# Two-layer hybrid decoder trunk: q first and four tiles wide, sixteen MLP tiles on unnormalised input, and 512-column matmuls that join the two halves of x in the last layer

## The chip, the cores and the metric

The kernel runs on one core of a Trainium2 chip. The time is the device time of one execution in microseconds (us); three executions of the kernel before were timed. One more execution was taken with the hardware profiler, and all rows below come from it.

## The reference, cut to what matters

Sixteen meta tokens and 256 tokens (272 positions, 2048 wide, float32) are normalised and go through two layers. The meta tokens are dropped at the end, so that the last layer computes 256 positions where it can.

```python
def hybrid_layer(h, ...):
    z = h @ in_proj                                   # 2048 x 6656
    q, k, v, u, g = split(z)                          # 1024, 256, 256, 1024, 4096 columns
    g_attn, g_ssm = split(sigmoid(g + gate_b))
    y_attn = sliding_window_attention(q, k, v, bias, sinks)
    y_ssm = s5_mixer(u, ...)                          # scan over time, gelu, y * sigmoid(y @ w_glu)
    mixed = (g_attn * (y_attn @ w_attn_up) + g_ssm * (y_ssm @ w_ssm_up)) @ w_out
    h = layer_norm(DN_ALPHA * h + mixed, ln_mix_g, ln_mix_b)
    f = square(relu(h @ w_mlp_up)) @ w_mlp_down       # 2048 -> 8192 -> 2048
    return layer_norm(DN_ALPHA * h + f, ln_mlp_g, ln_mlp_b)
```

## The kernel before, in words

Activations lie transposed: a tile holds 128 features on the partitions and the positions along the free axis, 16 tiles `H0..H15` for a width of 2048. To keep float32 accuracy with the faster matmul type, each operand is split in a rounded high part and the low rest. A product is three matmuls that add up in one PSUM bank: high weights by high x, high weights by low x, low weights by high x. The high and the low part of x lie in one tile, a row of positions apart.

`gemm` (line 408) cuts a product into steps. A step loads 512 KB of weights (1024 columns per partition) on SP's queue, ScalarE copies the high part `wh`, VectorE subtracts it from the loaded weights to get the low part `wo` (`split`, line 368), and TensorE runs 24 matmuls. Three pairs `wh`, `wo` are in turn, so that the split for a step begins when TensorE has left the step three before it. `wide` is how many output tiles of 128 features one group of steps fills: with 2, a step covers two output tiles and four of the contraction tiles k; with 4, four output tiles and two k. All output tiles of a group keep a bank until the last k. When an output tile is complete, its `evac` generator empties the bank, and the bank is free again when the generator's first reader has been issued (`self.free(p)`).

Six banks go round among the products (`BANKS`), and up to three of them may be held by side work, attention and the state-space branch (`SIDE`). The order of instructions on every engine is written out by a planner at build time: each piece of work is a generator that says on which engine and when it could go on (estimated times), the planner takes the earliest, and evacuations go before weight splits, weight splits before layer norm and side work.

The products of a layer, in order: u (line 1472 or 1474, four wide), k, q, v (1498 to 1500, two wide), the attention gate (1516), attn_up (1527), 28 of 32 steps of the state-space gate `gs` (1526), glu (1548), the rest of `gs`, ssm_up (1563, four wide), w_out (1582), and for each half of the 8192 hidden features mlp_up (1605, 1607, 1612, four wide) and mlp_down (in the last layer `down_tok`, line 1664, with tokens as weights and 512 columns of w_mlp_down as the moving operand). Attention runs beside the attention gate and must be over before attn_up; the state-space branch runs beside it from u on and must be over before glu.

Two layer norms are hidden behind products on unnormalised input. `ln_add` makes tiles `XG` of x times the norm's gain before the statistics are there, u of the second layer and the first eight tiles of mlp_up read these, and `deferred` (928) repairs their output with the statistics afterwards: a multiplication, which frees the bank, and an addition on VectorE. Meanwhile `ln_put` (910) writes the sixteen normalised tiles, each with two VectorE passes, a high copy on ScalarE and a low subtraction on VectorE. The product after it waits for these tiles one by one.

In the last layer `residual_tok` (1644) turns the residual to token order with 32 transposes and eight ScalarE copies; it starts a new pair only while at most two banks are held (line 1650), and `down_tok` lets it finish at line 1672.

Of the kernel before, what the change touches and what calls it, by code (L numbers as in the profile page):

```python
# [14 lines left out]
ALU = mybir.AluOpType  # L15
# [7 lines left out]
KT = D // 128  # L23
# [5 lines left out]
C_Q, C_K, C_V, C_U, C_GA, C_GS = 0, 1024, 1280, 1536, 2560, 4608  # L29
# [7 lines left out]
NCH = FF // 2 // 128  # L37
# [11 lines left out]
def fr(t, off, dims):  # L49
    return bass.AP(t.tensor, t.offset + off, [list(t.ap[0])] + [list(d) for d in dims])  # L50
# [131 lines left out]
class Builder:  # L182
# [222 lines left out]
        yield  # L405


    def gemm(self, w, c0, ms, nk, xs, n, evac, wide=2, r0=0, pre=None):

        steps, ms = [], list(ms)  # L410
        for g in range(0, len(ms), wide):
            group = ms[g:g + wide]
            ku = 8 // len(group)
            ps = {}
            for k0 in range(0, nk, ku):
                r, c = r0 + 128 * k0, c0 + 128 * group[0]
                src = w[r:r + 128 * ku, c:c + 128 * len(group)].rearrange("(k p) c -> p k c", p=128)

                def need(k0=k0, ku=ku):
                    for k in range(k0, k0 + ku):  # L420
                        xs(k)

                def mm(whi, wlo, k0=k0, ku=ku, ps=ps, group=group):
                    for j, m in enumerate(group):
                        if k0 == 0:
                            ps[m] = self.psum()
                        p, c = ps[m][:, :n], slice(128 * j, 128 * j + 128)
                        for i in range(ku):
                            k = k0 + i
                            hi, lo = xs(k)  # L430
                            self.mm(p, whi[:, i, c], hi, k == 0, False)
                            self.mm(p, whi[:, i, c], lo, False, False)
                            self.mm(p, wlo[:, i, c], hi, False, k == nk - 1)
                        if k == nk - 1:
                            self.own(evac(m, p), self.FIRST, p)

                steps.append(Step(src, (ku, 128 * len(group)), mm, need, pre if not steps else None))
        return steps
# [998 lines left out]
    def layer(self, l, prev):  # L1437
        nc, V, A, a = self.nc, self.V, self.A, self.a
        last = l == DEPTH - 1
        T0 = N_META if last else 0  # L1440
        n = NT - T0
        ts = slice(T0, NT)
        xh = lambda k: (self.H[k][:, 0, :NT], self.H[k][:, 1, :NT])
        xt = lambda k: (self.H[k][:, 0, ts], self.H[k][:, 1, ts])
        w_in = a["in_proj"][l]
        ctx = {}
        steps = []
# [45 lines left out]
        def ev_q(m, p):  # L1493
            yield self.after("act")
            A.activation(out=q_tile(m)[:, 0, ts], in_=p, func=AF.Copy, scale=0.125)
            self.free(p)

        steps += self.gemm(w_in, C_K, range(2), KT, xh, NT, ev_k)
        steps += self.gemm(w_in, C_Q, range(8), KT, xt, n, ev_q)
        steps += self.gemm(w_in, C_V, range(2), KT, xh, NT, ev_v)  # L1500

        def attn_go():
# [4 lines left out]
        def ev_gate(store, base, gm):  # L1507
            def ev(m, p):
                yield self.after("act")
                if m // 2 not in store:  # L1510
                    store[m // 2] = self.t(f"{base[0]}{base[1] + m // 2}", [128, 2, NT])
                A.activation(out=store[m // 2][:, m % 2, ts], in_=p, func=AF.Tanh, bias=self.gate_b(l, gm + m), scale=0.5)
                self.free(p)
            return ev

        steps += self.gemm(w_in, C_GA, range(16), KT, xt, n, lambda m, p: ev_gate(self.GA, ("G", 0), 0)(m, p), pre=attn_go)

        ya = lambda k: (self.Y[k][:, 0, ts], self.Y[k][:, 1, ts])

# [82 lines left out]
        for c in range(2):  # L1602
            w_up = a["w_mlp_up"][l]
            if c == 0:
                steps += self.gemm(w_up, 0, range(8), KT, lambda k: self.xg(self.ln)(k), n + 2,
                                   lambda m, p: self.deferred(self.ln, ev_up2)(m, p), 4)
                more = self.gemm(w_up, 0, range(8, NCH), KT, xt, n, ev_up2, 4)
                if last:
                    more[0].pre = lambda: ctx.__setitem__("rt", self.start(self.residual_tok(XS, self.ln, ctx)))
                steps += more  # L1610
            else:
                steps += self.gemm(w_up, 4096, range(NCH), KT, xt, n, ev_up2, 4)
            clear = HID.clear
            if not last:
                def ev_down(m, p, c=c):
                    yield self.after("dve")
                    x = XS[m // 2][:, m % 2, :n]
                    if c == 0:
                        V.scalar_tensor_tensor(out=x, in0=x, scalar=ALPHA, in1=p, op0=ALU.mult, op1=ALU.add)
                        self.free(p)  # L1620
                    else:
                        if m == 0:
                            self.ln_begin(1, l, T0)
                        V.tensor_tensor(out=x, in0=x, in1=p, op=ALU.add)
                        self.free(p)
                        yield from self.ln_add(m, x)

                down = self.gemm(a["w_mlp_down"][l], 0, range(16), NCH, hid, n, ev_down, 2 if c else 4, r0=4096 * c)
                if c == 0:
                    down[16].pre = lambda: self.start(self.phase_table(l + 1))  # L1630
            else:
                down = self.down_tok(a["w_mlp_down"][l], l, c, hid, ctx)
            if c == 0:
                down[-1].mm = (lambda hi, lo, f=down[-1].mm: (f(hi, lo), clear()))
            steps += down
# [8 lines left out]
    def residual_tok(self, XS, s, ctx):  # L1644
        R = ctx["res"] = {}
        while s.get("done", 0) < KT:
            yield W
        for c in range(4):
            for t in range(2):
                while t == 0 and (self.room(self.banks, 2) is None or len(self.banks.held) > 2):  # L1650
                    yield W
                yield self.after("pe")
                p = ctx["rp", t] = self.psum(True)
                for j in range(4):
                    x = XS[2 * c + j // 2][:, j % 2, 128 * t:128 * t + 128]
                    self.P.transpose(p[:, 128 * j:128 * j + 128], x, self.ident)
            for t in range(2):
                yield self.after("act")
                p = ctx["rp", t]
                R[c, t] = self.t(f"G{2 * c + t}", [128, 512])  # L1660
                self.A.activation(out=R[c, t], in_=p, func=AF.Copy, scale=ALPHA)
                self.free(p)
# [163 lines left out]
```

## Time and profile before

| | us |
|---|---|
| median of 3 runs | 2728.31 (2727.61 to 2731.21) |
| profiled execution | 2727.87 |
| span of the profile, first to last instruction | 2725.8 |
| TensorE busy | 2686.1 (99%) |
| VectorE busy | 1856.8 (68%) |
| ScalarE busy | 1275.8 (47%) |
| mean granted TensorE clock | 0.997 |

PE is TensorE, PEld its weight loads, DVE VectorE, ACT ScalarE, POOL GpSimd and SP the queue that issues the loads. All instructions come from helpers, so that the line is L147 throughout and rows are told apart by the tiles' names: `wl` is a loaded weight tile, `wh` and `wo` its high and low part, `bank` a PSUM bank, `H` and `D` activation tiles (in the second layer the names of some are swapped), `G` gates and residual, `lnr` and `lnc` the statistics of a layer norm. A matmul's duration contains its pipeline; the pace of a stage is its length divided by its matmuls.

### The profile page before, as it was taken

The numbers are of one execution on the slowest core, as the hardware profiler recorded it, in microseconds if no ns is written. First come the engines' busy times: TensorE is split into PE (matmuls) and PEld (weight loads), VectorE is DVE, ScalarE is ACT, GpSimd is POOL, SyncE is SP. The second block draws the span as 40 slices with busy tenths as digits, with TensorE's granted clock in tenths as the row PEclk, the third lists the DMA queues.
The fourth block names the chain that finished last, engine by engine and source line by source line (L and its number), as shares of the span: only waits on it lengthen the run. The fifth ranks groups of instructions, "written<-read, shape, count | busy, mean of one in ns | idle before, by whom it ended". The sixth has DMA issues, their size and how long they took to land.

```text
span 2725.8 us, 52091 instructions
## 1 busy us (share of the span) xinstructions
PE 2686.1 (99%) x21234; PEld 2581.9 (95%) x21234; DVE 1856.8 (68%) x3293; ACT 1275.8 (47%) x2020; POOL 66.1 (2%) x143
## 2 busy tenths in 40 slices
PE   7999999999999999999999999999999999999997
PEld 6999999999999999999999989999999988999886
DVE  7889985678655766555568999457886544455545
ACT  4456444456543334444445564444565533444433
POOL 2200000000000000000004000000000000000000
PEclk9999999999999999999999999999999999999999
DMA  5654445555664666555556654555566555556653
GB/s 178 181 166 132 150 155 172 176 176 165 178 177 172 197 202 194 176 173 175 175 167 195 191 154 158 181 186 186 186 181 177 176 188 190 186 186 186 217 191 141
DMA packets 378775, 483.36 MB, mean 177 GB/s; under 512 B 49046, under 2 KB 240232, under 8 KB 378536
## 3 DMA queue, kind: packets, MB, share of 16 engines
q1 hardware_dynamic: 374440, 477.81, 55.8%
q8 instruction: 166, 2.72, 0.4%
q0 software_dynamic: 4096, 2.24, 0.3%
q14 instruction: 73, 0.60, 0.1%
HBM read 471.14 MB, written 6.60 MB: 175 GB/s over the span
## 4 chain that ended last, share of the span: by engine, by line
PE 97%; DVE 1%; ACT 1%; SPq 0%; issue 0%; DMA 0%; ACTq 0%; DVEq 0%
PE bank L147 97%; PE pair L147 1%; DVE G L147 0%; SPq L147 0%; ACT wh L147 0%; DVE D L147 0%; DMA D<-in_x 0%; DVE wo L147 0%; ACT H L147 0%; ACT fnw L147 0%; DVE H L147 0%; DVE fst L147 0%; ACT fro L147 0%; DVE erw L147 0%; DVE est L147 0%
## 5 line engine op out<-in xcount | busy, mean ns | idle before, releaser
L147 DVE TENSOR_TENSOR wo<-wl,wh 128x1024 fp32r<-128x1024 f32 x864 | 1056.3, 1224 | 811.3 <-ACT wh L147 803.5
L147 ACT CAST wh<-wl 128x1024 fp32r<-128x1024 f32 x864 | 906.8, 1050 | 1284.4 <-PE bank L147 1094.4
L147 PE MATMUL bank<-D,wh 128*128 128x256 f32 (+2 forms) x7296 | 1347.5, 286 | 4.9 <-DVE D L147 3.5
L147 PEld LDWEIGHTS bank<-D,wh 128*128 128x128 f32 x7296 | 1134.7, 189 | 11.1 <-DVE D L147 4.8
L147 PE MATMUL bank<-D,wo 128*128 128x256 f32 (+2 forms) x3648 | 1039.4, 285 | 0.0
L147 PE MATMUL bank<-H,wh 128*128 128x272 f32 (+3 forms) x4480 | 847.4, 289 | 0.0
L147 PEld LDWEIGHTS bank<-H,wh 128*128 128x128 f32 x4480 | 702.6, 189 | 4.5 <-ACT wh L147 1.0
L147 PEld LDWEIGHTS bank<-D,wo 128*128 128x128 f32 x3648 | 688.2, 189 | 0.0
L147 PE MATMUL bank<-H,wo 128*128 128x272 f32 (+3 forms) x2240 | 644.3, 288 | 0.0
L147 PEld LDWEIGHTS bank<-H,wo 128*128 128x128 f32 x2240 | 423.1, 189 | 0.0
L147 PE MATMUL bank<-wh,D 128*128 128x512 f32 x512 | 161.9, 395 | 0.0
L147 PE MATMUL bank<-wh,H 128*128 128x512 f32 x512 | 161.3, 394 | 0.0
L147 PEld LDWEIGHTS bank<-wh,D 128*128 128x128 f32 x512 | 96.2, 188 | 23.0
L147 PEld LDWEIGHTS bank<-wh,H 128*128 128x128 f32 x512 | 96.2, 188 | 22.2
L147 DVE TENSOR_TENSOR D<-D,D 128x272 f32<-128x272 f32 (+2 forms) x208 | 102.5, 509 | 1.3
L147 PE MATMUL bank<-wo,D 128*128 128x512 f32 x256 | 101.0, 394 | 0.0
L147 PE MATMUL bank<-wo,H 128*128 128x512 f32 x256 | 100.7, 393 | 0.0
L147 POOL DMA_DIRECT2D D<-D x128 | 63.0, 499 | 1404.9 <-ACT D L147 1392.1
L147 ACT ACTIVATE tmp<-bank 128x272 f32<-128x272 f32 (+1 forms) x128 | 49.8, 389 | 19.3 <-PE bank L147 18.6
L147 PEld LDWEIGHTS bank<-wo,D 128*128 128x128 f32 x256 | 48.1, 188 | 11.2
L147 PEld LDWEIGHTS bank<-wo,H 128*128 128x128 f32 x256 | 48.1, 188 | 11.2
L147 DVE TENSOR_TENSOR_SCAN D<-par,D 128x136 f32<-128x136 f32 x128 | 50.7, 427 | 0.6
(245 smaller groups left out, 1473.5 us busy)
## 6 DMA issues: line engine op xcount, KB each, us to landing
wl<-in_w_mlp_up SPq DMA_DIRECT2D x256, 512.0 KB, 3.7
wl<-in_w_mlp_down SPq DMA_DIRECT2D x256, 512.0 KB, 3.5
wl<-in_in_proj SPq DMA_DIRECT2D x208, 512.0 KB, 3.7
wl<-in_w_out SPq DMA_DIRECT2D x64, 512.0 KB, 3.3
wl<-in_w_attn_up SPq DMA_DIRECT2D x32, 512.0 KB, 3.3
wl<-in_w_ssm_up SPq DMA_DIRECT2D x32, 512.0 KB, 3.9
wl<-in_ssm_w_glu SPq DMA_DIRECT2D x16, 512.0 KB, 3.9
turns<-bias SPq DMA_DIRECT2D x16, 272.0 KB, 4.4
```

Of the source, the lines that this page charges most:

```text
L147: return fn(*a, **k)
```

## The change

1. `gemm` gets a flag `join`. Where it is on and n is 256 (only in the last layer), one matmul of 512 columns multiplies the high weights by the high and the low x together, into the left and the right half of a bank; the low weights by the high x still go to the left half. `joined` then copies the right half to a temporary tile on ScalarE and adds it to the left half on VectorE, in the bank, before the evacuation begins. q and the attention gate have the flag off; u, k, v and the early mlp_up tiles have other widths.
2. q comes before k, and four tiles wide instead of two, in both layers.
3. In the last layer sixteen instead of eight tiles of mlp_up are taken on unnormalised input.
4. `residual_tok` starts a pair in the first half of a group (`self.phase` is the share of k that is done), no longer by the number of banks held.

```diff
-    def gemm(self, w, c0, ms, nk, xs, n, evac, wide=2, r0=0, pre=None):
+    def gemm(self, w, c0, ms, nk, xs, n, evac, wide=2, r0=0, pre=None, join=True):
+        both = join and 2 * n == 512
+
+        def joined(m, p, q):
+            yield self.after("act")
+            t = self.tmp()[:, :n]
+            self.A.copy(t, q)
+            yield self.after("dve")
+            self.V.tensor_tensor(out=p, in0=p, in1=t, op=ALU.add)
+            self.free(t)
+            yield from evac(m, p)
...
+                    self.phase = k0 / nk
...
                             hi, lo = xs(k)
-                            self.mm(p, whi[:, i, c], hi, k == 0, False)
-                            self.mm(p, whi[:, i, c], lo, False, False)
+                            if both:
+                                two = fr(hi, 0, [[lo.offset - hi.offset, 2], [1, n]])
+                                self.mm(ps[m].rearrange("p (a b) -> p a b", a=2), whi[:, i, c], two, k == 0, False)
+                            else:
+                                self.mm(p, whi[:, i, c], hi, k == 0, False)
+                                self.mm(p, whi[:, i, c], lo, False, False)
                             self.mm(p, wlo[:, i, c], hi, False, k == nk - 1)
                         if k == nk - 1:
-                            self.own(evac(m, p), self.FIRST, p)
+                            self.own(joined(m, p, ps[m][:, n:2 * n]) if both else evac(m, p), self.FIRST, p)
...
+        steps += self.gemm(w_in, C_Q, range(8), KT, xt, n, ev_q, 4, join=False)
         steps += self.gemm(w_in, C_K, range(2), KT, xh, NT, ev_k)
-        steps += self.gemm(w_in, C_Q, range(8), KT, xt, n, ev_q)
         steps += self.gemm(w_in, C_V, range(2), KT, xh, NT, ev_v)
...
-        steps += self.gemm(w_in, C_GA, range(16), KT, xt, n, lambda m, p: ev_gate(self.GA, ("G", 0), 0)(m, p), pre=attn_go)
+        steps += self.gemm(w_in, C_GA, range(16), KT, xt, n, lambda m, p: ev_gate(self.GA, ("G", 0), 0)(m, p), pre=attn_go, join=False)
...
-                steps += self.gemm(w_up, 0, range(8), KT, lambda k: self.xg(self.ln)(k), n + 2,
+                early = 16 if last else 8
+                steps += self.gemm(w_up, 0, range(early), KT, lambda k: self.xg(self.ln)(k), n + 2,
                                    lambda m, p: self.deferred(self.ln, ev_up2)(m, p), 4)
-                more = self.gemm(w_up, 0, range(8, NCH), KT, xt, n, ev_up2, 4)
+                more = self.gemm(w_up, 0, range(early, NCH), KT, xt, n, ev_up2, 4)
...
-                while t == 0 and (self.room(self.banks, 2) is None or len(self.banks.held) > 2):
+                while t == 0 and (self.room(self.banks, 2) is None or self.phase > 0.5):
```

## Rows read from the trace of the kernel before

**Rows 1.** The page's first part: busy us of each engine, share, instructions.
```profile
PE 2686.1 (99%) x21234; PEld 2581.9 (95%) x21234; DVE 1856.8 (68%) x3293; ACT 1275.8 (47%) x2020; POOL 66.1 (2%) x143
```

**Rows 2.** Windows, one stage each: from:to length, busy us, clock, DMA, GB/s.
```profile
81.11:93.19 12.08, 12.08 (x98) 12.08 (x97) 10.17 (x32) 4.88 (x6) 11.27 (x24) 1.00 0.67 207
...
1453.58:1471.91 18.33, 15.35 (x98) 13.86 (x97) 14.65 (x29) 9.71 (x18) 15.82 (x33) 0.91 0.68 184
...
1730.92:1810.77 79.85, 79.85 (x674) 79.85 (x673) 34.73 (x29) 34.98 (x41) 0.00 (x0) 1.00 0.60 185
...
1844.83:1890.20 45.37, 45.37 (x387) 45.37 (x385) 33.08 (x56) 22.02 (x31) 0.00 (x0) 1.00 0.55 185
1890.20:1981.42 91.22, 91.22 (x773) 91.17 (x771) 74.14 (x126) 46.06 (x78) 0.00 (x0) 1.00 0.57 186
...
2028.39:2171.88 143.49, 141.58 (x1186) 140.83 (x1185) 89.50 (x133) 77.62 (x127) 0.00 (x0) 1.00 0.61 181
2171.88:2350.08 178.20, 178.20 (x771) 144.36 (x770) 81.90 (x72) 69.18 (x70) 0.00 (x0) 1.00 0.54 186
2350.08:2532.90 182.82, 182.82 (x1538) 182.82 (x1536) 98.64 (x124) 86.08 (x123) 0.00 (x0) 1.00 0.59 185
```

**Rows 3.** Timeline of TensorE, k of the second layer: start, us, instruction, [idle, releaser].
```profile
1461.13 0.39 PE L147 MATMUL bank<-D,wh 128*128 128x272 f32 x1 [0.57 <-ACT D L147]
1462.43 0.39 PE L147 MATMUL bank<-D,wh 128*128 128x272 f32 x1 [0.91 <-DVE D L147]
...
1469.35 0.66 PE L147 MATMUL bank<-D,wh 128*128 128x272 f32 x2
...
1470.03 0.66 PE L147 MATMUL bank<-D,wh 128*128 128x272 f32 x2
```

**Rows 4.** Windows of 3 us in the same stage, columns as in rows 2.
```profile
1469.00:1472.00 3.00, 3.00 (x15) 3.00 (x16) 0.29 (x1) 0.39 (x1) 2.61 (x7) 0.55 1.07 237
```

**Rows 5.** Timeline of VectorE: low parts of normalised tiles, and a repair of u.
```profile
1434.57 0.79 DVE L147 TENSOR_TENSOR D<-G,D 128x272 fp32r<-128x272 f32 x2
...
1452.68 0.43 DVE L147 TENSOR_TENSOR tmp<-bank,lnr 128x272 f32<-128x272 f32 x1
...
1457.61 0.44 DVE L147 TENSOR_TENSOR D<-G,D 128x272 fp32r<-128x272 f32 x1
...
1461.94 0.79 DVE L147 TENSOR_TENSOR D<-G,D 128x272 fp32r<-128x272 f32 x2
...
1468.24 0.44 DVE L147 TENSOR_TENSOR D<-G,D 128x272 fp32r<-128x272 f32 x1 [0.48 <-ACT D L147]
```

**Rows 6.** Timeline of TensorE, mlp_up of the last layer.
```profile
2043.05 0.38 PE L147 MATMUL bank<-D,wh 128*128 128x256 f32 x1 [0.20 <-ACT D L147]
...
2045.82 0.39 PE L147 MATMUL bank<-D,wh 128*128 128x256 f32 x1 [1.13 <-DVE D L147]
```

**Rows 7.** Timeline of VectorE: the last normalised tiles of that norm.
```profile
2050.61 0.76 DVE L147 TENSOR_TENSOR D<-G,D 128x256 fp32r<-128x256 f32 x2
```

**Rows 8.** Groups by form, ScalarE: count | busy us, mean ns of one | idle before.
```profile
L147 ACT ACTIVATE tmp<-bank 128x256 f32<-128x256 f32 x64 | 24.4, 382 | 8.6 <-PE bank L147 8.5
```

**Rows 9.** Groups by form, VectorE.
```profile
L147 DVE SCALAR_TENSOR_TENSOR G<-G,bank 128x256 f32<-128x256 f32 x16 | 6.7, 418 | 2.0 <-PE bank L147 2.0
```

**Rows 10.** Timeline of ScalarE where one group of four follows another (mlp_up).
```profile
2371.11 0.38 ACT L147 ACTIVATE tmp<-bank 128x256 f32<-128x256 f32 x1
...
2373.00 1.05 ACT L147 CAST wh<-wl 128x1024 fp32r<-128x1024 f32 x1 [0.21 <-PE bank L147]
```

**Rows 11.** Timeline of VectorE at the same place.
```profile
2371.24 1.23 DVE L147 TENSOR_TENSOR wo<-wl,wh 128x1024 fp32r<-128x1024 f32 x1 [1.62 <-ACT wh L147]
```

**Rows 12.** Attention's last products, by tile: count, ns min/median/max, first and last start.
```profile
L147 PE MATMUL bank<-H,vab x96: 272/273/324, 1569.7 to 1642.1; 128*64 128x128 f32 x96
```

**Rows 13.** The chain in order of time: the state-space branch's last input product.
```profile
1680.67 0.67 PE pair L147 x8
```

**Rows 14.** Groups by form, TensorE: the residual's transposes.
```profile
L147 PE MATMUL bank<-ident,G 128*128 128x128 f32 x32 | 3.7, 272 | 0.0
```

## The prediction, made before the change was built

> **What bounds the kernel now.** I read the page first, then windows laid on the stages, then the timeline where a stage is longer than its matmuls, last the rows of the two engines that feed TensorE. TensorE is busy for 2686 of 2725.8 us and VectorE for 68% [rows 1]: the time is the sum of matmuls, so I count matmuls and look for places where TensorE stands.
>
> A stage's length over its matmuls is the pace. With 256 columns, 28 steps of the state-space gate take 79.85 us for 672 matmuls (118.8 ns), ssm_up 45.37 for 384 (118.2), w_out 91.22 for 768 (118.8), the second mlp_up 182.82 for 1536 (119.0). With 512 columns, the first mlp_down of the last layer takes 178.20 us for 768 (232.0) [rows 2]. I use 118.7 and 232.0: 256 more columns cost 113.3 ns, so 256 columns cost 113.3 and each matmul some 5.4 ns more, whatever its width.
>
> TensorE stands in two places. k of the second layer takes 18.33 us, k of the first, the same 96 matmuls, 12.08 [rows 2]: 6.25 us are lost. The timeline shows how: matmuls wait for a normalised tile (0.57 us, 0.91 us, and so on) [rows 3], and then the granted clock is 0.55 for 3 us [rows 4], three matmuls taking 0.68 us (1469.35 to 1470.03) [rows 3], about twice their usual time; that is the level of 1.2 instead of 2.4 GHz after the idling. The second place is mlp_up of the last layer, where the first tiles on normalised input wait 0.20 and 1.13 us and once more between them [rows 6]. That stage has 1152 matmuls (137.1 us at 119.0) and 32 transposes (3.7 us) [rows 14], 140.8 of 143.49 [rows 2]: 2.7 us lost.
>
> **Part 1, joined matmuls.** Joined products in the last layer are gate 16 tiles by 16 k, attn_up 16 by 8, glu 8 by 8, ssm_up 16 by 8, w_out 16 by 16, mlp_up 16 by 16 and 32 by 16: 256 + 128 + 64 + 128 + 256 + 256 + 512 = 1600 pairs. Each pair of 256-column matmuls (237.4 ns) becomes one of 512 (232.0): 5.4 ns, in all 8.7 us less. No row shows a moving operand in two pieces; mlp_down's is one piece. Bounds: if the break costs as much as a matmul's start, nothing is gained; if each of the two pieces pays a start, 8.6 us are lost; if all 12 ns that a 256-column matmul takes beyond 256 columns at 2.4 GHz (106.7) go, 19 us are gained. I take 8.7, from the nearest row, 512 columns into the same kind of bank.
>
> The Trainium skill, page "TensorE: Matmul & The Clock Gate", section "Wait — 56ns, not 53.3ns?", puts the fixed cost of a warm matmul at 2.5 ns on top of its columns at 2.4 GHz. By it the 1600 pairs would give 4.0 us instead of 8.7, and the total below would be 2717.7. These rows disagree: 118.7 and 232.0 ns stand 12.0 and 18.7 above such columns [rows 2], so the measured paces decide.
>
> **What the join adds.** 16 + 16 + 8 + 16 + 16 + 16 + 32 = 120 tiles get a ScalarE copy of 256 columns, priced by its nearest row, an evacuation from a bank, 0.38 us [rows 8], and a VectorE addition, 0.42 us [rows 9] (bounds 0.3 to 0.8 us, as no row shows VectorE writing to a bank): 46 and 50 us of engine time. It lies beside matmuls. VectorE is busy 33.08 of 45.37 us in ssm_up and 74.14 of 91.22 in w_out [rows 2]; with 16 additions each (6.7 us) 39.8 of some 44.7 and 80.8 of some 89.8. These are the tightest stages, and the matmuls still last longer. At 0.8 us an addition ssm_up would hold VectorE 45.9 us, over 1 us too long.
>
> What can go late is a bank. With groups of four, two of six banks are free when a group ends; the new group's third tile needs that of the old group's first. In the second mlp_up the first group ends at 2350.08 + 192 x 0.119 = 2372.93, the third tile starts 12 matmuls on, at 2374.36. The old first tile was read at 2371.11, bank free at 2371.49 [rows 10]: 2.9 us early. Afterwards a copy (0.38) is done by 2371.49; the addition stands behind a split that runs from 2371.24 to 2372.47 [rows 11], so is done by about 2372.9; the read competes with a copy of weights at 2373.00 (1.05 us) [rows 10]. Ahead of it, the bank is free at 2373.3; behind it, at 2374.4, just late. There are 3 such boundaries in ssm_up, 3 in the joined part of the first mlp_up, 7 in the second: 13. I take 0.15 us each, 2 us; bounds 0 and 0.4 us each (5 us).
>
> **Part 2, q first, four wide.** k used four new tiles in 3 us; q uses two per step of 24 x 0.1187 = 2.85 us. After u ends at 1453.58 [rows 2], tile 11 (k = 10) is needed at step 5, 1467.8, tile 13 at 1470.7, tile 15 at 1473.5. The low parts, counted in order, give the tenth at 1458.05 (first and last of seven such rows shown), 11 and 12 at 1462.73, the sixteenth at 1468.68 [rows 5]: all 5 us early. So stall and half clock go: 6.25 us. k then finds all tiles. q needs four banks at once where u has just ended; its third tile starts 12 matmuls on, at 1455.0, and u's second bank is released at 1453.1 [rows 5], so nothing waits. Loads: q has 16 steps of 512 KB either way, in rows twice as long, moved past k's four loads on SP's queue, and issues nothing on POOL's; v and the attention start stay where they were, as the three products take the same time together. In the first layer k runs at full pace (12.08 us) [rows 2], so order alone gives nothing. Held banks rise from two to four during q, leaving two for side work; that hides in attention's end at 1642.1 [rows 12] against attn_up, which starts 384 x 0.1187 = 46 us before the state-space gate's 1730.92 [rows 2], near 1685, and in the branch's last input product at 1681 [rows 13] against glu after 1810.77 [rows 2]. Without that cover, each microsecond late would be one of the path. Bounds 0 and 6.25 us.
>
> **Part 3, sixteen early tiles.** They run some 46 us longer on unnormalised input, until about 2074; the last normalised tiles are ready at 2051.4 [rows 7]. The 2.7 us go. Eight tiles by 48 = 384 matmuls are 258 wide instead of 256: 2 x 0.443 x 384 = 0.3 us. Their repair, two more VectorE passes on each of eight tiles (0.42 each [rows 9]), 7 us, hides in that stage's 54 idle VectorE us [rows 2]. Bounds 0 and 2.7.
>
> **Part 4, residual.** 32 transposes come earlier and stay as many; their 3.7 us [rows 14] are paid there as here. Their two banks in the first half of a group hinder nothing that the second half needs. Zero, bounds -0.5 and +0.5.
>
> **Sum.** -8.7 - 6.25 - 2.7 + 0.3 + 2.0 = -15.35 us. The profiled execution took 2727.87 (span 2725.8 and 2.1 around it), the median is 2728.31, 0.4 more: 2712.5 and 2713.0. I say 2713.
>
> **Rivals.** (B) *Two pieces cost two starts*: the join pays nothing, the stalls go all the same. For it: no row has a moving operand in pieces; against: nothing in the rows charges for pieces, and 512 columns run at 232. 2713 + 8.7 = 2721.7.
> (D) *The normalised tiles stay late*: VectorE follows u's repairs, so that the tiles shift with q. For it: VectorE is busy 14.65 of 18.33 us there [rows 2]; against: 5 us of reserve. 2713 + 6.25 = 2719.3.
> (C) *The bank takes the stall's place*, slower than before: at each of the 13 boundaries the addition stands behind a split and the read behind a copy of weights, and both again because other tiles' passes come first. One split and one copy beyond the reserve are 1.23 + 1.05 = 2.28 us [rows 10, 11], at 13 boundaries 30 us: 2713 - 2 + 30 = 2741. It decides from (15.35 + 2.0) / 13 = 1.3 us a boundary. For it: one such pair uses up the reserve already; against: evacuations go ahead of splits in the planner.
> (E) *All the overhead goes with the matmul*: 19.2 us instead of 8.7, 2702.5.
>
> **How the numbers follow.** What a measurement here can tell from no change is 0.2%, 5.5 us, so faster means below 2722.8. Chances: forecast 0.56 (0.53 faster, 0.03 same), B 0.14 (half and half, as it lies at the bound), D 0.12 (0.11 and 0.01), E 0.08, C 0.10 (0.09 slower, 0.01 same). Faster 0.79, same 0.12, slower 0.09. The range takes E in below and reaches past B above, with the banks' 5 us and the worse bounds in part: 2702 to 2725.
>
> **What would show it.** Right: in the last layer a pair of 512 and 256 columns every 350 ns; q of the second layer starts with no wait, and no window at half clock before the end; mlp_up's first normalised tile without a wait; at 13 boundaries gaps under half a microsecond. Wrong: a 512-column matmul in the joined products above 237 ns (B) or below 226 (E); waits of q on tiles of layer norm (D); idle time before a group's third tile, released by ScalarE or VectorE reading a bank (C); or new waits of TensorE on attention, which I leave as they are.

## The result and the profile after

The changed kernel takes 2714.42 us (median of 6 runs, 2713.35 to 2716.49), the kernel before 2729.43; the ratio is 0.9945, 95% interval 0.9932 to 0.9958. Forecast were 2713 and 15.35 us less; the medians differ by 15.0. The profiled execution took 2714.52 us, its span is 2712.7, 13.1 less than the span before.

The page's first part answers to [rows 1]: 1600 matmuls fewer, VectorE and ScalarE each some 40 us busier.

```profile
PE 2679.0 (99%) x19634; PEld 2503.7 (92%) x19634; DVE 1898.5 (70%) x3421; ACT 1315.7 (49%) x2156; POOL 66.3 (2%) x143
```

Windows of the changed kernel by stage of the last layer, each from its first matmul to the next stage's first; columns as in [rows 2]. In order: q, k, v, attention gate, attn_up, 28 steps of the state-space gate, ssm_up, w_out, the sixteen early mlp_up tiles, the other sixteen, the first mlp_down, the second mlp_up (glu and the last steps of the gate, between 1803.38 and 1837.04, are left out).

```profile
1454.77:1506.24 51.47, 51.21 (x458) 50.14 (x457) 45.60 (x93) 28.28 (x51) 15.86 (x33) 1.00 0.71 207
1506.24:1521.27 15.03, 15.03 (x164) 14.21 (x162) 13.92 (x28) 7.37 (x14) 0.00 (x0) 1.00 0.61 172
1521.27:1536.09 14.82, 14.82 (x154) 14.17 (x148) 14.50 (x29) 6.67 (x12) 0.00 (x0) 1.00 0.59 187
1536.09:1676.39 140.30, 139.40 (x1423) 129.91 (x1419) 132.22 (x370) 80.54 (x199) 0.00 (x0) 1.00 0.60 166
1676.39:1724.82 48.43, 48.43 (x347) 41.81 (x346) 43.93 (x82) 24.23 (x38) 0.00 (x0) 1.00 0.55 173
1724.82:1803.38 78.56, 78.56 (x450) 68.63 (x449) 39.95 (x44) 38.34 (x54) 0.00 (x0) 1.00 0.61 188
1837.04:1881.93 44.89, 44.89 (x259) 39.30 (x258) 36.86 (x67) 26.79 (x46) 0.00 (x0) 1.00 0.59 185
1881.93:1972.18 90.25, 90.25 (x516) 78.93 (x515) 79.78 (x145) 51.70 (x95) 0.00 (x0) 1.00 0.61 188
1972.18:2065.29 93.11, 93.11 (x775) 93.00 (x773) 80.16 (x147) 63.54 (x124) 0.00 (x0) 1.00 0.63 182
2065.29:2159.67 94.38, 94.38 (x547) 82.16 (x546) 55.91 (x80) 53.35 (x92) 0.00 (x0) 1.00 0.63 179
2159.67:2337.80 178.13, 178.13 (x771) 144.26 (x770) 85.88 (x82) 69.90 (x73) 0.00 (x0) 1.00 0.61 189
2337.80:2519.76 181.96, 181.96 (x1025) 157.37 (x1024) 107.99 (x152) 93.54 (x151) 0.00 (x0) 1.00 0.64 185
```

The stages of the kernel before that [rows 2] does not hold: q, v, attention gate, attn_up, eight early tiles.

```profile
1471.91:1527.01 55.10, 55.10 (x537) 52.92 (x535) 49.58 (x104) 27.12 (x50) 0.00 (x0) 1.00 0.63 183
1527.01:1542.13 15.12, 15.12 (x164) 14.30 (x162) 14.80 (x29) 6.51 (x14) 0.00 (x0) 1.00 0.59 172
1542.13:1684.23 142.10, 140.03 (x1447) 130.07 (x1442) 135.79 (x376) 80.45 (x196) 0.00 (x0) 1.00 0.57 163
1684.23:1730.92 46.69, 46.69 (x426) 46.36 (x425) 32.19 (x49) 18.36 (x20) 0.00 (x0) 1.00 0.55 181
1981.42:2028.39 46.97, 46.97 (x391) 46.86 (x389) 40.73 (x76) 30.98 (x60) 0.00 (x0) 1.00 0.63 180
```

The reader is to take sums over stages that end at the same matmul, since side work moves between neighbours:

| stretch | before | after | difference |
|---|---|---|---|
| up to the end of u, second layer | 1453.58 | 1454.77 | +1.2 |
| q, k, v, attention gate, attn_up | 277.34 | 270.05 | -7.3 |
| state-space gate to w_out | 250.50 | 247.36 | -3.1 |
| first mlp_up | 190.46 | 187.49 | -3.0 |
| mlp_down, second mlp_up, mlp_down | 539.13 | 538.44 | -0.7 |
| after the last matmul starts | 14.8 | 14.6 | -0.2 |

The +1.2 is the first product (u of the first layer), which starts beside the first loads: it took 59.7 to 60.9 us over all the profiles here, whatever the order of q and k. No other stage of the first layer differs by more than 0.6 us.

### The profile page after: what moved, and what is told of

Same layout as the page of the kernel before. It is cut to its first block, busy times and chain, and to the rows that moved or that the text cites. A ratio compares the mean times of both kernels' runs of the same rounds, so it can differ in the third digit from the quotient of the medians.

```text
span 2712.7 us, 49216 instructions
## 1 busy us (share of the span) xinstructions
PE 2679.0 (99%) x19634; PEld 2503.7 (92%) x19634; DVE 1898.5 (70%) x3421; ACT 1315.7 (49%) x2156; POOL 66.3 (2%) x143
## 4 chain that ended last, share of the span: by engine, by line
PE 98%; DVE 0%; ACT 0%; SPq 0%; DMA 0%; issue 0%; ACTq 0%
PE bank L147 97%; PE pair L147 1%; DVE G L147 0%; SPq L147 0%; DMA D<-in_x 0%; ACT fnw L147 0%; ACT H L147 0%; DVE D L147 0%; DVE fst L147 0%; ACT fro L147 0%; ACT vm L147 0%; ACT wh L147 0%; DVE erw L147 0%; DVE est L147 0%; ACT frs L147 0%
## 5 line engine op out<-in xcount | busy, mean ns | idle before, releaser
L147 PE MATMUL bank<-D,wh 128*128 128x272 f32 (+3 forms) x5696 | 1293.8, 314 | 0.0
L147 PE MATMUL bank<-D,wo 128*128 128x256 f32 (+2 forms) x3520 | 1002.3, 285 | 0.0
L147 PEld LDWEIGHTS bank<-D,wh 128*128 128x128 f32 x5696 | 933.8, 189 | 65.4 <-ACT tmp L147 2.2
L147 PE MATMUL bank<-H,wh 128*128 128x272 f32 (+3 forms) x4480 | 893.9, 296 | 0.0
L147 PEld LDWEIGHTS bank<-H,wh 128*128 128x128 f32 x4480 | 712.6, 189 | 15.8 <-ACT wh L147 1.0
L147 PE MATMUL bank<-H,wo 128*128 128x272 f32 (+3 forms) x2368 | 680.9, 288 | 0.0
L147 PEld LDWEIGHTS bank<-D,wo 128*128 128x128 f32 x3520 | 663.3, 188 | 0.1
L147 PEld LDWEIGHTS bank<-H,wo 128*128 128x128 f32 x2368 | 448.1, 189 | 0.0
L147 PEld LDWEIGHTS bank<-wo,D 128*128 128x128 f32 x256 | 48.1, 188 | 11.6 <-DVE wo L147 0.4
L147 ACT COPY tmp<-bank 128x256 f32<-128x256 f32 x120 | 44.5, 371 | 16.1 <-PE bank L147 15.1
```

Source lines behind the costliest of these rows:

```text
L147: return fn(*a, **k)
```

## The experiments

Each edit is made to the changed kernel. Most stages repeat to some 0.05 us between profiles of kernels that don't differ there; u of the first layer, q and the attention gate of the second and the last mlp_down differ by 0.4 to 1.2 us. So stages tell apart what the whole time, which scatters by 1 to 2 us, cannot.

**The join off.**

```diff
-        both = join and 2 * n == 512
+        both = False
```

> The changed kernel with the join off everywhere: three 256-column matmuls per pair again, no copy and addition; q first, the sixteen early tiles and the residual's test stay. Theory (each removed matmul saves its fixed 5.4 ns, 1600 of them, and the additions cost some 2 us in bank waits): 8.7 - 2 = 6 to 7 us slower than the changed kernel, about 2721, and no gap before the third tile of a group in mlp_up. Rival (two pieces cost two starts, the gain came from the stalls alone): within 2 us of the changed kernel. Rival (the additions cost more than the join gains): faster than the changed kernel.

Measured: 2721.27 us (2718.8 to 2722.0), 0.9967 of the kernel before (0.9954 to 0.9979). Windows of the second mlp_up, of the attention gate, and of 3 us within the gate:

```profile
2343.87:2526.70 182.83, 182.83 (x1538) 182.82 (x1537) 98.61 (x124) 86.07 (x123) 0.00 (x0) 1.00 0.61 185
1535.92:1678.49 142.57, 141.19 (x1423) 131.46 (x1420) 132.31 (x370) 80.40 (x199) 0.00 (x0) 0.99 0.59 163
...
1546.00:1549.00 3.00, 3.00 (x14) 3.00 (x15) 2.96 (x12) 0.38 (x2) 0.00 (x0) 0.50 1.01 268
```

The whole is 6.8 us slower, as the theory has it, but 2.3 of that is the attention gate, which is not joined: TensorE waits 0.35 and then 0.50 us before matmuls of attention near its start, where the changed kernel has only the first wait, and the clock then goes to half (0.50 above; 1.00 throughout in the changed kernel). Over the joined stages the join gives 4.9 us: state-space gate 79.84 to 78.56 and 11.39 to 11.23, attn_up 48.82 to 48.43, glu 22.67 to 22.43, ssm_up 45.37 to 44.89, w_out 91.22 to 90.25, first mlp_up 94.91 to 94.38, second 182.83 to 181.96. Per pair that is 5.7 ns in the gate (224 pairs), 3.75 in ssm_up and w_out, only 1.7 in the second mlp_up.

**q after k, two wide.**

```diff
+        steps += self.gemm(w_in, C_K, range(2), KT, xh, NT, ev_k)
+        steps += self.gemm(w_in, C_Q, range(8), KT, xt, n, ev_q, join=False)
-        steps += self.gemm(w_in, C_Q, range(8), KT, xt, n, ev_q, 4, join=False)
-        steps += self.gemm(w_in, C_K, range(2), KT, xh, NT, ev_k)
```

> The changed kernel with q after k and two wide again, as before. Theory (k of the second layer catches up with the normalised tiles, idles and loses the clock): 6.3 us slower than the changed kernel, about 2720.7, with a window at half clock and k at about 18 us. Rival (the stall only moves into attention's waits, which take as much): within 2 us of the changed kernel.

Measured: 2722.02 us (2720.97 to 2723.47), 0.9974 (0.9963 to 0.9984). The window of k:

```profile
1453.93:1472.32 18.39, 15.43 (x98) 13.84 (x97) 14.67 (x29) 9.70 (x18) 15.84 (x33) 0.91 0.65 183
```

18.39 us at a clock of 0.91, as [rows 2] had 18.33. From u's end to attn_up's end it takes 277.1 us, 7.0 more than the changed kernel: the 6.25 expected and under 1 us, with TensorE idle for 2.0 us in the attention gate instead of 0.9.

**q first, two wide.**

```diff
-        steps += self.gemm(w_in, C_Q, range(8), KT, xt, n, ev_q, 4, join=False)
+        steps += self.gemm(w_in, C_Q, range(8), KT, xt, n, ev_q, 2, join=False)
```

> The changed kernel with q first, but two wide: a step then takes four new tiles in 2.85 us, as k did in 3. Theory (what counts is that four wide uses tiles at half the rate): the stall comes back in q, 4 to 6.5 us slower than the changed kernel, about 2719 to 2721. Rival (the order alone did it, since q has more work than k): within 2 us of the changed kernel.

Measured: 2723.62 us (2721.89 to 2725.47), 0.9976 (0.9967 to 0.9986). Windows of q, and of 3 us after its waits; then two of the waits in TensorE's timeline:

```profile
1454.40:1515.22 60.82, 57.16 (x525) 53.96 (x523) 53.79 (x112) 30.75 (x59) 15.78 (x33) 0.97 0.65 182
...
1469.00:1472.00 3.00, 3.00 (x17) 3.00 (x18) 2.14 (x9) 0.69 (x3) 3.00 (x7) 0.64 0.92 277
```

```profile
1462.95 0.39 PE L147 MATMUL bank<-D,wh 128*128 128x256 f32 x1 [0.91 <-DVE D L147]
...
1468.98 0.38 PE L147 MATMUL bank<-D,wh 128*128 128x256 f32 x1 [0.91 <-DVE D L147]
```

The stall, its releaser and the low clock are those of k before [rows 3, 4], now in q. From u's end to attn_up's end it takes 278.9 us, 8.8 more than the changed kernel, where 4 to 6.5 were expected, and 1.5 more than the kernel before. TensorE is idle for 3.7 us in q, against 3.0 in k before [rows 2]; where the rest comes from was not traced. So the order alone gives nothing; taking two new tiles a step instead of four does.

**Eight early tiles.**

```diff
-                early = 16 if last else 8
+                early = 8
```

> The changed kernel with eight instead of sixteen mlp_up tiles on unnormalised input in the last layer. Theory (the wait on normalised tiles comes back, 2.7 us, but eight more tiles are joined, 128 pairs by 5.4 ns = 0.7 us, and 384 matmuls are two columns narrower, 0.3 us): 1.7 us slower than the changed kernel, about 2716, with gaps of 2 to 3 us in all at the start of the first mlp_up on normalised tiles. Rival (the wait was hidden by something else): 1 us faster than the changed kernel.

Measured: 2722.29 us (2717.46 to 2723.11), 0.9969 (0.9956 to 0.9981): some 8 us slower where 1.7 was expected. The first mlp_up on normalised tiles and 3 us within it, then TensorE's timeline there:

```profile
2019.80:2167.74 147.94, 143.58 (x802) 124.05 (x801) 93.49 (x148) 83.55 (x147) 0.00 (x0) 0.98 0.60 171
...
2034.00:2037.00 3.00, 3.00 (x9) 2.54 (x10) 3.00 (x10) 1.71 (x5) 0.00 (x0) 0.50 0.64 178
```

```profile
2033.87 0.79 PE L147 MATMUL bank<-D,wh 128*128 128x512 f32 x1 [2.22 <-DVE D L147]
2034.45 0.42 PE L147 MATMUL bank<-D,wo 128*128 128x256 f32 x1
...
2046.45 0.50 PE L147 MATMUL bank<-D,wh 128*128 128x512 f32 x1 [2.14 <-DVE D L147]
```

Both parts of mlp_up take 194.93 us, 7.4 more than in the changed kernel. Where the unjoined matmuls waited in small pieces, the first for a high part from ScalarE (0.20 us, [rows 6]), a joined one stands 2.2 us twice, both times for VectorE, and in this run the clock went to half after each (0.50 granted in the stretch shown). Not every execution seems to lose it: one of five, at a mean granted clock of 0.998 instead of 0.997, took 2717.46 us.

The joined matmul needs the low part, the last to be written, together with the high one. ScalarE and VectorE before the first wait ends:

```profile
2031.17 1.05 ACT L147 CAST wh<-wl 128x1024 fp32r<-128x1024 f32 x1 [1.49 <-PE bank L147]
2032.12 0.40 ACT L147 CAST D<-G 128x256 fp32r<-128x256 f32 x1
...
2032.25 1.22 DVE L147 TENSOR_TENSOR wo<-wl,wh 128x1024 fp32r<-128x1024 f32 x1
2033.39 0.42 DVE L147 TENSOR_TENSOR D<-G,D 128x256 fp32r<-128x256 f32 x1
```

The high part was there at 2032.52, the low part, behind a weight split, at 2033.81, and the matmul started at 2033.87. An unjoined matmul could have started 1.3 us earlier, but only one, since the next needs the low part. So most of the wait is the tile's own delay. It is the tenth of the sixteen normalised tiles: its low part came 14.0 us after the stage began, in the kernel before 11.6, written there together with the ninth:

```profile
2039.26 0.75 DVE L147 TENSOR_TENSOR D<-G,D 128x256 fp32r<-128x256 f32 x2
```

In this run its high copy stands behind a copy of weights that had waited 1.49 us for TensorE. Why the planner's order came out so was not tried.

**The attention gate joined too.**

```diff
-ev_gate(self.GA, ("G", 0), 0)(m, p), pre=attn_go, join=False)
+ev_gate(self.GA, ("G", 0), 0)(m, p), pre=attn_go)
```

> The changed kernel with the join on in the attention gate of the last layer too (16 tiles by 16 k, 256 pairs), beside attention and the state-space branch, where VectorE is busy 135.8 of 142 us. Theory (attention ends 40 us before it is needed, so VectorE's lateness is hidden): 256 x 5.4 ns = 1.4 us faster than the changed kernel, about 2713. Rival (16 additions of 0.42 us on a full VectorE hold up weight splits and banks): 2 us slower or more, with gaps on TensorE in that stage.

Measured: 2718.23 us (2717.87 to 2719.45), 0.9956 (0.9944 to 0.9969). Windows of the attention gate, the state-space gate and 3 us within the first, then the longest wait in TensorE's timeline:

```profile
1535.72:1678.61 142.89, 140.02 (x1158) 116.78 (x1154) 132.34 (x372) 84.61 (x213) 0.00 (x0) 0.99 0.58 160
1726.74:1806.78 80.04, 80.04 (x491) 69.68 (x490) 42.05 (x50) 39.46 (x57) 0.00 (x0) 1.00 0.59 184
...
1626.00:1629.00 3.00, 2.83 (x20) 2.42 (x22) 2.52 (x15) 0.59 (x3) 0.00 (x0) 0.61 0.53 175
```

```profile
1626.17 1.06 PE L147 MATMUL bank<-H,H 64*128 64x272 f32 x3 [1.53 <-ACT H L147]
```

The rival's time holds; its mechanism is shown in part only. With 256 matmuls fewer the stage is 2.6 us longer. TensorE is idle for 2.9 us instead of 0.9, always before a matmul of the side work; the longest ends as ScalarE has copied a part of attention out of a bank, and the clock falls after it (0.61). Whether that matmul waited for the copy or for the bank the trace does not say; no wait is put down to a weight split. And side work slides on: 41 more matmuls stand in the state-space gate, 1.5 us more. So beside attention the join costs 3 to 4 us, and the reserve of attention's end does not hide it, since the gaps are within the stage. That the copies and additions delay attention's own passes fits this, but no run took them apart.

**The sum to the temporary tile.**

```diff
-            self.V.tensor_tensor(out=p, in0=p, in1=t, op=ALU.add)
-            self.free(t)
-            yield from evac(m, p)
+            self.V.tensor_tensor(out=t, in0=p, in1=t, op=ALU.add)
+            self.free(p)
+            yield from evac(m, t)
```

> The changed kernel, where the addition writes the sum to the temporary tile instead of into the bank, so that the bank is free after the addition, not after the read that follows it. Theory (at each group of four in mlp_up the third tile waits 0.15 us for a read that stands behind a copy of weights): these waits go, 11 x 0.15 = 1.7 us faster than the changed kernel, about 2712.7, and the second mlp_up falls from 181.97 to about 180.5 us. Rival (the gap is something else that a new group of four brings): no difference, 181.9 in that stage.

Measured: 2716.12 us (2715.65 to 2716.2), 0.9947 (0.9934 to 0.9961): by the medians 1.7 us slower than the changed kernel where 1.7 faster was expected. Windows of the second mlp_up, w_out and the early tiles, then two waits in TensorE's timeline:

```profile
2340.90:2521.65 180.75, 180.75 (x1025) 157.45 (x1024) 107.92 (x152) 94.51 (x151) 0.00 (x0) 1.00 0.63 187
1881.89:1973.84 91.95, 90.34 (x517) 78.96 (x515) 80.34 (x145) 51.38 (x95) 0.00 (x0) 1.00 0.58 183
1973.84:2068.91 95.07, 93.48 (x774) 93.12 (x773) 80.50 (x148) 63.60 (x124) 0.00 (x0) 1.00 0.61 178
```

```profile
1893.09 0.50 PE L147 MATMUL bank<-D,wh 128*128 128x512 f32 x1 [1.61 <-DVE D L147]
...
2000.97 0.48 PE L147 MATMUL bank<-H,wh 128*128 128x258 f32 x2 [1.59 <-DVE tmp L147]
```

Where it was meant to help it does, by 1.2 us in the second mlp_up. But w_out and the early tiles each get a wait of 1.6 us for VectorE. The first is for the low part of a tile that w_out reads, the second for a pass of VectorE that empties a bank. The temporary tiles are now held longer, and the planner's order differs; which of these brings the waits was not tried.

**mlp_up two wide.**

```diff
-                more = self.gemm(w_up, 0, range(early, NCH), KT, xt, n, ev_up2, 4)
+                more = self.gemm(w_up, 0, range(early, NCH), KT, xt, n, ev_up2, 2 if last else 4)
...
-                steps += self.gemm(w_up, 4096, range(NCH), KT, xt, n, ev_up2, 4)
+                steps += self.gemm(w_up, 4096, range(NCH), KT, xt, n, ev_up2, 2 if last else 4)
```

> The changed kernel with the joined mlp_up tiles of the last layer two wide instead of four, so that four of six banks are free when a group ends. Theory (bank waits): the gap before the third tile of a group is gone, the second mlp_up takes 180.5 us or less, 1.5 to 2 us faster than the changed kernel. Rival (the pace of 235 instead of 232 ns there comes from the tiles read and not from banks): 181.5 to 182, no difference beyond 0.5 us.

Measured: 2711.23 us (2709.97 to 2712.49), 0.9929 (0.9917 to 0.9942), faster than both kernels. Windows of the first mlp_up on normalised tiles and of the second:

```profile
2065.59:2158.97 93.38, 93.38 (x547) 81.98 (x546) 58.30 (x85) 54.74 (x96) 0.00 (x0) 1.00 0.61 181
2337.08:2516.69 179.61, 179.61 (x1025) 156.90 (x1024) 109.97 (x157) 94.47 (x155) 0.00 (x0) 1.00 0.62 188
```

3.4 us less in the two stages, more than the bank waits: the second mlp_up is at 175.4 ns a matmul, the pace of ssm_up (44.89 us for 256) and of the gate, and a pair gains 6.3 ns there. No weight load waits for ScalarE's read of a bank in this stage any more. With this, the join is worth 8.3 us over all stages against the run without it, which has mlp_up four wide; mlp_up two wide without the join was not tried.

**The join alone.** The second and fourth edits together.

```diff
-        steps += self.gemm(w_in, C_Q, range(8), KT, xt, n, ev_q, 4, join=False)
         steps += self.gemm(w_in, C_K, range(2), KT, xh, NT, ev_k)
+        steps += self.gemm(w_in, C_Q, range(8), KT, xt, n, ev_q, join=False)
...
-                early = 16 if last else 8
+                early = 8
```

> The kernel before with the join alone (and the residual's test): q after k and two wide, eight early tiles. Sum of the prediction's terms for this part: 8.7 - 2 = 6.7 us faster than before, about 2723.5. Theory after the runs so far (the joined products gain 4.9 us, but the wait on normalised tiles in mlp_up is longer, in one piece, and brings a stretch at half clock, some 4.5 us): the same as before within 1.5 us, about 2729.5, with k of the second layer at 18.4 us and the first mlp_up on normalised tiles near 148.

Measured: 2726.16 us (2724.8 to 2729.84), 0.9989 (0.998 to 0.9998), between the two times expected. Windows of mlp_up on normalised tiles, and of 3 us after the first wait there:

```profile
2025.51:2170.35 144.84, 140.48 (x802) 121.46 (x801) 93.49 (x148) 83.42 (x147) 0.00 (x0) 1.00 0.60 175
...
2040.00:2043.00 3.00, 3.00 (x19) 2.52 (x18) 3.00 (x9) 2.17 (x5) 0.00 (x0) 1.00 0.62 177
```

This stage is idle for 4.4 us, as with eight early tiles above (4.4), but the clock stayed at full, and it is 3.1 us shorter. So both runs with a join and eight early tiles have the long waits, and one of them the half clock after them; what decides that stays open. Of the 6.7 us that the prediction's terms give the join, some 3.8 are left by the medians when it stands alone (0.5 to 5.5 by the interval).

## Why the prediction was right

**The sum, 15.35 us.** Measured 15.0 by medians, 13.1 by the two profiles, 1.2 of whose difference lies in the first product. By stages the join gave 4.9 us instead of 6.7, part 2 gave 7.0 instead of 6.25 and part 3 2.5 instead of 2.4, 14.4 in all: one term was too large and another too small. That the medians come within 0.4 us of the forecast is luck; the interval allows 11.5 to 18.6.

**Part 1, 8.7 us, and its bank waits, 2.0.** The mechanism was right and the net too large: 4.9 us measured against 6.7. Two pieces cost nothing extra. The joined matmul has the pace of mlp_down's: of 44.89 us for 256 matmuls in ssm_up, half of them 256 wide at some 118.5 ns, 232 ns are left for the other half. What was mis-sized is, first, the pace before, taken as 118.7 throughout: ssm_up ran at 118.2, and so did w_out without the side work's matmuls in it (0.44 us), and they gain 3.75 ns a pair. A joined pair takes 350.7 ns in ssm_up, in the gate and in mlp_up two wide alike, and three unjoined matmuls took 354.5, 356.4 and, four wide, 357.1 ns there: how much the join saves depends on the pace before. Second, mlp_up four wide: its pairs are slower than elsewhere beyond the bank waits, and two wide they are not. Each joined pair also saves one weight load, 1600 of them like the matmuls (PEld x21234 to x19634); the runs don't tell the two apart.

The Trainium skill's 2.5 ns for a matmul's fixed cost ("TensorE: Matmul & The Clock Gate", section "Wait — 56ns, not 53.3ns?") lies below the 3.75 to 6.3 ns that a removed matmul with its weight load gave here where no bank wait takes part of it; the measurement decides.

**The additions' price** was right: 0.37 us for a copy and 0.43 us for an addition into a bank, in groups by form of the changed kernel:

```profile
L147 DVE TENSOR_TENSOR bank<-bank,tmp 128x256 f32<-128x256 f32 x120 | 48.1, 425 | 0.0
...
L147 ACT COPY tmp<-bank 128x256 f32<-128x256 f32 x120 | 44.5, 371 | 16.1 <-PE bank L147 15.1
```

**The bank waits, 13 by 0.15 us.** The place and the size were right in mlp_up: seven such waits in the second, three in the first, some 0.22 us each. ssm_up has none. The timeline of the second mlp_up, ScalarE first, then a weight load of TensorE:

```profile
2360.48 1.05 ACT L147 CAST wh<-wl 128x1024 fp32r<-128x1024 f32 x1 [0.22 <-PE bank L147]
2361.43 0.93 ACT L147 ACTIVATE tmp<-bank 128x256 f32<-128x256 f32 x3
...
2361.86 0.19 PEld L147 LDWEIGHTS bank<-D,wh 128*128 128x128 f32 x1 [0.22 <-ACT tmp L147]
```

The third tile's first weight load waits 0.22 us for the read, which stands behind the copy of weights, the order that the prediction worked out. Taking the wait away gave 1.2 us for seven boundaries, 0.17 each.

**Part 2, 6.25 us.** 7.0 measured, and the reason, two tiles a step instead of four, is shown by the run with q first and two wide. Without the join the same stages gain only 5.1 us (272.3 against 277.3), with the stretch at half clock in the attention gate.

**Part 3, 2.7 us less 0.3.** In the changed kernel the first mlp_up has no wait. Without the join the early tiles give 2.5 us there (190.46 to 188.00), as forecast; in the two runs with eight early tiles beside a join these tiles are worth 4.3 and 7.4 us. The terms were added up as if the parts were independent, and these two are not: part 3 is what keeps part 1 from paying more for the late tiles.

**Part 4, zero.** The transposes now stand near the start of the first mlp_up's normalised part (2073.7 to 2099.9), which has no idle time (94.38 of 94.38); undoing it alone was not tried.

Of the rivals, B and E are excluded by the joined pace, D by q at full clock without a wait on layer norm, C by its size: 0.22 us of wait a boundary where 1.3 was needed.

## What to carry to other kernels

Where weight-stationary matmuls of half a bank share their weights, one full-bank matmul saved 3.75 to 6.3 ns here, with the extra copy and addition hidden beside matmuls. Beside attention, with VectorE 94% busy, the same edit cost 3 to 4 us. A product that consumes late tiles should take few of them per step. Consumers joined over two parts of a tile wait for the later part, and where the order of the other engines is laid out anew, look at when the tiles come before you blame the consumer. When a bank is held longer, check how many are free when a group ends: narrower groups gave 3.4 us here.

## What the runs showed of the hardware

A stall's price is not its length. Waits for the normalised tiles cost 2.7 us in three small pieces (the kernel before), 4.4 us of idle time in two long waits with the clock at full (the join alone), and the same idle time plus some 3 us with the clock at 0.50 in the stretch after (eight early tiles). In the run without the join two waits of 0.35 and 0.50 us came before a stretch at 0.50; the first alone, in the changed kernel, left the clock at 1.00. And the joined pairs of mlp_up ran at 177.7 ns a matmul four wide, 176.5 without the bank waits, 175.4 two wide, on the same tiles; what makes the remaining 1.1 ns was not settled.
